# A hybrid state-space and conformer trunk: tables, backward scan, gates and z projections put into one hand-written TensorE order

## The chip, the cores and the metric

The kernel runs on one core of a Trainium2 chip. The metric is the time of one execution on the device in microseconds; the median of several runs is given. Every duration below is from one profiled execution. The engines are TensorE (PE in the rows, its weight loads PEld), VectorE (DVE), ScalarE (ACT) and GpSimd (POOL); SP issues most transfers.

## What is computed

Two layers run over 1024 latent tokens and 256 context tokens, 1024 features wide. The change lies in layer 0, whose mixer is this, cut to what matters:

```python
z, xbc, dt, glu, gate = split(h @ w_in)         # h: modulated tokens
# state-space branch, 16 heads, chunks of 128 tokens, 10 chunks in all
a_cum = cumsum(dt * a)                           # the tables, forward and backward
states = einsum(bc, exp(a_cum[-1] - a_cum), x*dt)
h_in = scan(h * exp(a_cum[-1]) + states)         # one scan forward, one backward
y = y_diag + y_off + flip(...) + x * d_skip
ya = rms_norm(y * silu(z))
# convolution branch
yb = silu(layer_norm(dwconv(val * sigmoid(gt), 31 taps))) * silu(gate)
out = concat([ya, yb]) @ w_out
```

## The kernel before

Each projection in 32-bit precision is three matmuls of a high and a low part: ScalarE casts the high part of a weight tile from its raw load (line 158: `wh`, `zh`, `woh`, `yh`), a subtraction on VectorE (line 159) makes the low part. Raw tiles (`wr`) have two buffers, which z weights and gate weights share.

The place is the end of `inproj0`. Up to there stand the glu and convolution-input projections, the early gates 4 to 7 (their Silu goes to DRAM as `gs_d`), and the long 31-tap convolution on GpSimd and VectorE. Then, in the program's order:

- `zblocks((0, 1))`: two of three blocks of the z and dt projection, ten token tiles each. Every tile of 352 columns takes 24 matmuls; between tiles stand transposes of conv output (`token_major`) and one modulation row at a time (`mod_row`, eight small matmuls on line 1308).
- `gate(2)`: one channel block of the gate projection, 72 matmuls over slices of 512, 512 and 256 tokens; ScalarE applies Silu (line 1384), GpSimd multiplies by the convolution output (line 1385).
- At the same time the conformer's normalisation (lines 928 to 939: statistics, eight subtractions on VectorE, eight activations), and the early gates: for each, `gs_d` is loaded into the one buffer `gse` (line 1331), multiplied on GpSimd (line 1332) and stored in three pieces (line 1334).
- `dt_prep`: the tables. A polynomial for dt on VectorE, `da` (line 1448), cumsum matmuls (lines 1453 to 1456), exponentials, casts into `xparts`, two sets of ten transposes (line 1495) and two transfers of the result (line 1497).
- `ssd_back`: the backward scan over ten chunks. For each, `xtok` is loaded (line 1511), scaled on VectorE (line 1515), multiplied in four `bst` matmuls (line 1535), added to the state (line 1539) and stored (line 1526).
- `zblocks((2,))`: the third z block. Its pool of split weights (`zp`) is opened after the pool with `gse` was closed and lies on the same memory.
- gates 3, 0 and 1, with loads of output weights `wb` (line 1406) after each, and the load and split of the first tile of the gated convolution (`yl0`, `yh0`, `ylo0`, line 1410 on).

Behind it `split_wo` casts seven output weights from `wb` and one from `xl`, and the forward scan runs interleaved with the output projection (line 1003).

A scheduler orders the instructions of each engine by its own estimates and by priorities, so the order in the program is not in every place that of an engine: in the kernel before, the scan matmuls and the z matmuls are mixed by it.

Of the kernel before, what the change touches and what calls it, by code (L numbers as in the profile page):

```python
# [90 lines left out]
def run(steps):  # L91

    for _ in steps:
        pass
# [16 lines left out]
class Kern:  # L111
# [1074 lines left out]
    def inproj0(self, hhi, hlo, cv, xbc_d, zs_d, gs_d, dtr, vwh, yb_d, xt_d, hb_d, s0, first):  # L1186
# [161 lines left out]
        def zblocks(js):  # L1348
            todo = [(c, h) for c in (1, 0, 9, 8, 7, 6, 5, 4, 3, 2) for h in range(2)]
            with ExitStack() as ez:  # L1350
                xq = ez.enter_context(self.pool(name="xq", bufs=2)) if js[0] < 2 else None
                zp = ez.enter_context(self.pool(name="zp", bufs=4))
                for j in js:
                    w = [self.load_w(zp, A["wzdt"][j, q], [P, 2, 352], "z", raw=(wp, "wr", [P, 8, P], 2)) for q in range(4)]
                    for t in range(NT):
                        ps = self.bank("mm")
                        ts = slice(t * P, (t + 1) * P)
                        self.mm3(ps[:, :352], (lambda k: hhi[:, k, ts], lambda k: hlo[:, k, ts]),
                                 (lambda k: w[k // 2][0][:, k % 2], lambda k: w[k // 2][1][:, k % 2]), range(8))
                        n = j * NT + t  # L1360
                        if 3 <= n < 2 * NT:
                            for _ in range(2 if n % 6 == 5 else 1):
                                token_major(xq, *todo.pop(0))
                        if mods:
                            layer, m, d, plus = mods.pop(0)
                            mod_row(layer, m, (23 - len(mods)) % 16)
                            if len(mods) == 8:
                                mod_turn(16, ((0, 16, self.gcol[:, 0], 0.0), (1, 0, self.mod1[:, 0], 0.0)))
                            elif not mods:
                                mod_turn(8, ((1, 8, self.mod1[:, 1], 1.0),))  # L1370
                        zs = tq.tile([P, 512], F32, name="zs", tag="th")
                        if j == 0:
                            nc.scalar.copy(dtr[:, t], ps[:, :32])
                            nc.scalar.activation(zs[:, :320], ps[:, 32:352], AF.Silu)
                            nc.sync.dma_start(zs_d[t, :, :320], zs[:, :320])
                        else:
                            nc.scalar.activation(zs[:, :352], ps[:, :352], AF.Silu)
                            nc.sync.dma_start(zs_d[t, :, 352 * j - 32:352 * j + 320], zs[:, :352])
                assert not xq or not todo

        def gate(i):
# [5 lines left out]

            self.proj_ch(wp, W[28 + i], hhi, hlo, ev)

        zblocks((0, 1))  # L1390
        gate(2)
        ecf.close()
        self.s0 = s0.__enter__()
        self.dt_prep(dtr)
        self.ssd_back(xt_d, hb_d)
        zblocks((2,))
        em.close()

# [3 lines left out]
        k = 0  # L1402
        for i, m in ((3, 3), (0, 5), (1, 7)):
            gate(i)
            for k in range(k, m):
# [10 lines left out]
    def dt_prep(self, dtr):  # L1416
# [3 lines left out]
        with ExitStack() as e:  # L1420
# [26 lines left out]
            for d in range(2):  # L1447
                nc.vector.scalar_tensor_tensor(
                    da[:, d], dt[:, :, 16 * d:16 * d + 16], -1.0,
                    ea[:, None, 16 * d:16 * d + 16].broadcast_to([P, NT, 16]), op0=ALU.mult, op1=ALU.mult)  # L1450
            ps = self.bank("ms")
            fl = da.rearrange("p d c h -> p d (c h)")
# [26 lines left out]
            for X, dst, quad in ((Ac, self.rA_d, False), (bias, self.rB_d, True)):  # L1479
# [8 lines left out]
                nc.vector.tensor_tensor(o(2).bitcast(FR), v(rem), o(1), op=ALU.subtract)  # L1488
                xq = xp.rearrange("p c t h -> p (c t h)")
                rt = q.tile([96, NT, P], F32, name="rt", tag="rt")  # L1490
                for j0 in range(0, NT, 4):
# [9 lines left out]
    def ssd_back(self, xt_d, hb_d):  # L1501
# [3 lines left out]
        with ExitStack() as e:  # L1505
# [15 lines left out]
            for i, c in enumerate(order):  # L1521
                xt, xs = nxt
                if i < len(order) - 1:
                    nxt = prep(order[i + 1])
# [157 lines left out]
```

## Time and profile before

| | us |
|---|---|
| median of 3 runs (2162.4 to 2163.54) | 2163.49 |
| the profiled execution's own time | 2159.51 |
| its span in the profile | 2157.5 |
| TensorE busy in the span | 2050.3 |

The span is what the profile shows from the first to the last instruction; 2.0 us of the execution's own time lie around it. Idle time of an engine matters only where the engines behind it wait for it; TensorE, busy 95% of the span, is the one on which most idle time counts.

### The profile page before, as it was taken

Reading aid. Unit: us, or ns where it says so; the run is one execution under the profiler, and the core shown is the slowest. Engines: PE = TensorE matmul, PEld = TensorE weight load, DVE = VectorE, ACT = ScalarE, POOL = GpSimd, SP = SyncE. Lnnn points to the kernel's source line nnn. Section 1 sums busy time; section 2 is a strip of 40 time slices with the busy share of each in tenths; the row PEclk is TensorE's granted clock in tenths of the full one; section 3 lists DMA queues with packets and bytes.
Section 4 is the critical chain, followed back from the end, with each engine's and each line's share of the span. In section 5 each row is a group of like instructions: output and inputs, shape, how many; then the busy total and the mean of one; then the engine's idle time right before and its main releaser. Section 6 shows DMA issues by size and latency. Waiting matters only on the chain. (4 is left out here: it accounts for less than half of the span.)

```text
span 2157.5 us, 28255 instructions
## 1 busy us (share of the span) xinstructions
PE 2050.3 (95%) x10636; PEld 1631.5 (76%) x10636; DVE 1344.7 (62%) x1889; ACT 990.9 (46%) x1549; POOL 980.0 (45%) x646
## 2 busy tenths in 40 slices
PE   7999999999995999999899999999999998899896
PEld 6888888889873876665588788888777776677675
DVE  6788897758454335678776221422566766676676
ACT  7455667543362132224233333333666877655510
POOL 0198999800222235556421114823345555434562
PEclk9999999999996999999899999999999999999998
DMA  8011122235756645555343322522312111533463
GB/s 311 30 40 33 47 87 79 88 131 191 234 161 203 241 144 176 179 190 175 120 147 113 129 71 98 186 83 84 101 48 67 51 47 48 157 112 115 145 179 127
DMA packets 156976, 268.01 MB, mean 124 GB/s; under 512 B 18677, under 2 KB 97393, under 8 KB 156585
## 3 DMA queue, kind: packets, MB, share of 16 engines
q1 hardware_dynamic: 155416, 262.69, 37.0%
q0 software_dynamic: 1280, 3.26, 0.5%
q8 instruction: 83, 1.36, 0.3%
q14 instruction: 53, 0.43, 0.1%
q10 hardware_dynamic: 144, 0.26, 0.0%
HBM read 189.17 MB, written 76.94 MB: 123 GB/s over the span
## 5 line engine op out<-in xcount | busy, mean ns | idle before, releaser
L1236 POOL TENSOR_TENSOR accq<-accq,prod 128x1295 f32<-128x1295 f32 x90 | 287.7, 3197 | 33.9 <-ACT prod L1235 17.2
L171 PE MATMUL m<-hhi,wh 128*128 128x512 f32 (+1 forms) x792 | 280.9, 355 | 1.8 <-ACT th L1279 0.9
L171 PE MATMUL m<-hlo,wh 128*128 128x512 f32 (+1 forms) x792 | 280.6, 354 | 0.0
L171 PE MATMUL m<-hhi,wl 128*128 128x512 f32 (+1 forms) x792 | 280.2, 354 | 0.0
L1244 DVE SCALAR_TENSOR_TENSOR acc<-u,vwh,acc 128x1295 f32<-128x1295 f32 x150 | 235.1, 1568 | 12.9 <-ACT acc L1241 9.7
L171 PE MATMUL m<-h1hi,wh 128*128 128x512 f32 (+1 forms) x544 | 213.2, 392 | 1.7 <-ACT rb L423 1.4
L733 POOL TENSOR_TENSOR pl<-pt,ph 128x512 fp32r<-128x512 f32 x96 | 129.3, 1349 | 186.2 <-ACT ph L732 178.7
L171 PE MATMUL m<-h1lo,wh 128*128 128x512 f32 (+1 forms) x544 | 213.0, 392 | 0.0
L171 PE MATMUL m<-h1hi,wl 128*128 128x512 f32 (+1 forms) x544 | 212.1, 390 | 0.0
L1003 PE MATMUL m<-wol,yh 128*128 128x512 f32 x448 | 182.1, 406 | 1.3 <-DVE wol L956 1.1
L1003 PE MATMUL m<-woh,yh 128*128 128x512 f32 x448 | 181.4, 408 | 1.8 <-ACT yh L158 0.9
L1003 PE MATMUL m<-woh,ylo 128*128 128x512 f32 x448 | 182.0, 406 | 0.3 <-DVE ylo L159 0.3
L1235 ACT ACTIVATE prod<-u,vwh 128x1295 f32<-128x1295 f32 x90 | 124.1, 1381 | 97.9 <-POOL accq L1236 95.6
L171 PEld LDWEIGHTS m<-hhi,wh 128*128 128x128 f32 x792 | 149.7, 189 | 24.1 <-ACT th L1279 1.6
L171 PEld LDWEIGHTS m<-hhi,wl 128*128 128x128 f32 x792 | 149.7, 189 | 20.8
L171 PEld LDWEIGHTS m<-hlo,wh 128*128 128x128 f32 x792 | 149.8, 189 | 20.6
L159 POOL TENSOR_TENSOR wl<-wr,wh 128x1024 fp32r<-128x1024 f32 x33 | 81.5, 2471 | 117.2 <-ACT wh L158 95.2
L732 ACT CAST ph<-pt 128x512 fp32r<-128x512 f32 x152 | 93.1, 619 | 81.5 <-PE po L740 70.4
L740 PE MATMUL po<-ph,vs 128*66 128x512 f32 x304 | 122.0, 401 | 3.8 <-ACT yo L745 3.8
L171 PEld LDWEIGHTS m<-h1hi,wh 128*128 128x128 f32 x544 | 102.7, 189 | 22.9 <-ACT rb L423 2.0
L171 PEld LDWEIGHTS m<-h1hi,wl 128*128 128x128 f32 x544 | 102.6, 189 | 21.0 <-issue 0.2
L171 PEld LDWEIGHTS m<-h1lo,wh 128*128 128x128 f32 x544 | 102.8, 189 | 19.7
(371 smaller groups left out, 4765.6 us busy)
## 6 DMA issues: line engine op xcount, KB each, us to landing
wr<-in_wch_dram SPq DMA_DIRECT2D x69, 512.0 KB
mw<-in_modw_dram SPq DMA_DIRECT2D x24, 512.0 KB
mr<-in_modw_dram SPq DMA_DIRECT2D x16, 512.0 KB
wor<-in_wout_dram SPq DMA_DIRECT2D x16, 512.0 KB
xbc_d<-acc SPq DMA_DIRECT2D x12, 640.0 KB
xcT<-xbc_d SPq DMA_DIRECT2D x20, 320.0 KB
xt_d<-xtok SPq DMA_DIRECT2D x20, 320.0 KB
xtok<-xt_d SPq DMA_DIRECT2D x10, 640.0 KB
```

Of the source, the lines that this page charges most:

```text
L159: (nc.gpsimd if pool_lo else nc.vector).tensor_tensor(lo, src, hi.bitcast(F32), op=ALU.subtract)
L171: nc.tensor.matmul(out, x(k), y(k), start=(c == 0), stop=(c == tot - 1))
L732: nc.scalar.copy(ph, p)
L733: (nc.gpsimd if x in (0, 1, 3) else nc.vector).tensor_tensor(pl, p, ph.bitcast(F32), op=ALU.subtract)
L740: nc.tensor.matmul(po[:66], vs[:, kb, v], p[y], start=first and i == 0, stop=last and i == 2)
L1003: nc.tensor.matmul(ps[f], y[u][:, k], w[k][v][:, 512 * f:512 * f + 512], start=i + j == 0, stop=i + j == 9)
L1235: nc.scalar.activation(pr, u[:, k:k + N], AF.Copy, scale=vwh[:, i, k:k + 1])
L1236: nc.gpsimd.tensor_tensor(acc, acc, pr, op=ALU.add)
L1244: nc.vector.scalar_tensor_tensor(acc[:, :N], u[:, k:k + N], vwh[:, i, k:k + 1], acc[:, :N], op0=ALU.mult, op1=ALU.add)
```

## The change

The stretch from gate 2 on gets a TensorE order written by hand (`manual_schedule` for that engine alone); the other engines stay with the scheduler. `zblocks`, `gate`, `dt_prep` and `ssd_back` become generators that hand back how many columns they have issued. `fill` yields the matmuls of gate 2, gate 3, then z block 2's weight loads, gate 0, and z block 2; `ahead` draws so many columns from it between the steps of the tables (15000, 16000, or up to the end of a gate) and of the backward scan (11700 for each chunk). Gate 1 stands behind. The modulation rows are drawn two at a time after each fifth tile of z blocks 0 and 1, and the turn of the last eight rows (`mod_turn`) comes after gate 2's matmuls. Loads of all seven `wb` come after gate 1. From line 1390 or so on, lines of the changed kernel stand 27 to 31 lower (the table transposes of line 1495 are line 1524, scan matmuls of line 1535 line 1565).

```diff
--- before.py
+++ after.py
@@ -1352,22 +1352,22 @@
                 zp = ez.enter_context(self.pool(name="zp", bufs=4))
                 for j in js:
                     w = [self.load_w(zp, A["wzdt"][j, q], [P, 2, 352], "z", raw=(wp, "wr", [P, 8, P], 2)) for q in range(4)]
+                    yield 0
                     for t in range(NT):
                         ps = self.bank("mm")
                         ts = slice(t * P, (t + 1) * P)
-                        self.mm3(ps[:, :352], (lambda k: hhi[:, k, ts], lambda k: hlo[:, k, ts]),
-                                 (lambda k: w[k // 2][0][:, k % 2], lambda k: w[k // 2][1][:, k % 2]), range(8))
+                        yield from self.mm3_(ps[:, :352], (lambda k: hhi[:, k, ts], lambda k: hlo[:, k, ts]),
+                                             (lambda k: w[k // 2][0][:, k % 2], lambda k: w[k // 2][1][:, k % 2]), range(8))
                         n = j * NT + t
                         if 3 <= n < 2 * NT:
                             for _ in range(2 if n % 6 == 5 else 1):
                                 token_major(xq, *todo.pop(0))
-                        if mods:
-                            layer, m, d, plus = mods.pop(0)
-                            mod_row(layer, m, (23 - len(mods)) % 16)
-                            if len(mods) == 8:
-                                mod_turn(16, ((0, 16, self.gcol[:, 0], 0.0), (1, 0, self.mod1[:, 0], 0.0)))
-                            elif not mods:
-                                mod_turn(8, ((1, 8, self.mod1[:, 1], 1.0),))
+                        for _ in range(2 if n % 5 == 4 and n < 20 else 1):
+                            if mods:
+                                layer, m, d, plus = mods.pop(0)
+                                mod_row(layer, m, (23 - len(mods)) % 16)
+                                if len(mods) == 8:
+                                    mod_turn(16, ((0, 16, self.gcol[:, 0], 0.0), (1, 0, self.mod1[:, 0], 0.0)))
                         zs = tq.tile([P, 512], F32, name="zs", tag="th")
                         if j == 0:
                             nc.scalar.copy(dtr[:, t], ps[:, :32])
@@ -1385,23 +1385,50 @@
                 nc.gpsimd.tensor_tensor(gt[:, :b - a], cv[i][:, a:b], gt[:, :b - a], op=ALU.mult)
                 nc.sync.dma_start(yb_d[a][i], gt[:, :b - a])
 
-            self.proj_ch(wp, W[28 + i], hhi, hlo, ev)
-
-        zblocks((0, 1))
-        gate(2)
+            return self.proj_ch_(wp, W[28 + i], hhi, hlo, ev)
+
+        run(zblocks((0, 1)))
         ecf.close()
         self.s0 = s0.__enter__()
-        self.dt_prep(dtr)
-        self.ssd_back(xt_d, hb_d)
-        zblocks((2,))
-        em.close()
+        with tc.manual_schedule(engines={mybir.EngineType.PE}):
+            def fill():
+                for i in (2, 3):
+                    yield from gate(i)
+                    yield None
+                z = zblocks((2,))
+                next(z)
+                yield from gate(0)
+                yield from z
+
+            def ahead(cols):
+                while cols > 0:
+                    c = next(oth, None)
+                    if c is None:
+                        return
+                    cols -= c
+
+            oth = fill()
+            dt = self.dt_prep(dtr)
+            next(dt)
+            ahead(15000)
+            mod_turn(8, ((1, 8, self.mod1[:, 1], 1.0),))
+            em.close()
+            ahead(99999)
+            next(dt)
+            ahead(16000)
+            next(dt)
+            ahead(99999)
+            run(dt)
+            for _ in self.ssd_back(xt_d, hb_d):
+                ahead(11700)
+            run(oth)
 
         ewl = self.ewl = ExitStack()
         wl = ewl.enter_context(self.pool(name="wl", bufs=1, side="right"))
         wb = [(k, wl.tile([P, D], F32, name=f"wb{k}", tag=f"wb{k}"), (wl, f"wb{k}")) for k in range(1, 8)]
         k = 0
-        for i, m in ((3, 3), (0, 5), (1, 7)):
-            gate(i)
+        for i, m in ((1, 7),):
+            run(gate(i))
             for k in range(k, m):
                 nc.sync.dma_start(wb[k][1], A["wout0"][9 + k])
             k = m
@@ -1448,6 +1475,7 @@
                 nc.vector.scalar_tensor_tensor(
                     da[:, d], dt[:, :, 16 * d:16 * d + 16], -1.0,
                     ea[:, None, 16 * d:16 * d + 16].broadcast_to([P, NT, 16]), op0=ALU.mult, op1=ALU.mult)
+            yield
             ps = self.bank("ms")
             fl = da.rearrange("p d c h -> p d (c h)")
             nc.tensor.matmul(ps[:, 0:160], self.tu, fl[:, 0], start=True, stop=True)
@@ -1487,6 +1515,7 @@
                 nc.scalar.copy(o(1).bitcast(FR), v(rem))
                 nc.vector.tensor_tensor(o(2).bitcast(FR), v(rem), o(1), op=ALU.subtract)
                 xq = xp.rearrange("p c t h -> p (c t h)")
+                yield
                 rt = q.tile([96, NT, P], F32, name="rt", tag="rt")
                 for j0 in range(0, NT, 4):
                     n = min(4, NT - j0)
@@ -1520,6 +1549,7 @@
             H = None
             for i, c in enumerate(order):
                 xt, xs = nxt
+                yield
                 if i < len(order) - 1:
                     nxt = prep(order[i + 1])
                 if H is not None:
```

No instruction of arithmetic is added or taken away; their orders on the engines are what differs. At three places:

TensorE at the tables and the start of the backward scan, before. `ms<-da` are the cumsums, `ms<-cs,xparts` the transposes of the tables, `ms<-cs,gcol` small matmuls that turn gate columns to rows, `bst` the scan, `m<-zh,hhi` z block 2:

```order
L1453 MATMUL ms<-da,cs 128x160
L1454 MATMUL ms<-da,cs 128x160
L1456 MATMUL ms<-da,cs 128x320
L1495 MATMUL ms<-cs,xparts 96x128 x20
L222 MATMUL ms<-cs,gcol 128x128 x8
L1535 MATMUL bst<-xtok 128x512 x6
L171 MATMUL m_5857<-zh,hhi 128x352
L171 MATMUL m_5895<-zh,hhi 128x352
```

And after, from gate 3's last matmuls (`m_5810`) on; `m_5900` is gate 0:

```order
L171 MATMUL m_5810<-hhi,wl 128x256
L171 MATMUL m_5810<-hhi,wh 128x256
L171 MATMUL m_5810<-hlo,wh 128x256
L171 MATMUL m_5810<-hhi,wl 128x256
L1524 MATMUL ms<-cs,xparts 96x128 x10
L222 MATMUL ms<-cs,gcol 128x128 x8
L171 MATMUL m_5900<-hhi,wh 128x512
L171 MATMUL m_5900<-hlo,wh 128x512
L171 MATMUL m_5900<-hhi,wl 128x512
L171 MATMUL m_5900<-hhi,wh 128x512
L171 MATMUL m_5900<-hlo,wh 128x512
```

The second set of transposes now has all of gate 3 ahead of it, and gate 0 stands ahead of the first scan matmul. Z block 2 starts only after gate 0 and among the scan.

GpSimd behind the convolution, before. `gs` are gate multiplications (`u_782` is gate 2, `u_783` gate 3), `gse` those of the early gates, `Hb` the backward scan's state:

```order
L1385 TENSOR_TENSOR gs<-u_782,gs 128x256
L1332 TENSOR_TENSOR gse<-u_784,gse 128x1280
L1332 TENSOR_TENSOR gse<-u_785,gse 128x1280
L1332 TENSOR_TENSOR gse<-u_786,gse 128x1280
L1332 TENSOR_TENSOR gse<-u_787,gse 128x1280
L1531 TENSOR_TENSOR Hb<-Hb,expS 128x1024 x4
```

And after:

```order
L1385 TENSOR_TENSOR gs<-u_782,gs 128x512
L1332 TENSOR_TENSOR gse<-u_784,gse 128x1280
L1385 TENSOR_TENSOR gs<-u_782,gs 128x256
L1385 TENSOR_TENSOR gs<-u_783,gs 128x512
L1332 TENSOR_TENSOR gse<-u_785,gse 128x1280
L1385 TENSOR_TENSOR gs<-u_783,gs 128x512
L1385 TENSOR_TENSOR gs<-u_783,gs 128x256
L1332 TENSOR_TENSOR gse<-u_786,gse 128x1280
L1332 TENSOR_TENSOR gse<-u_787,gse 128x1280
```

The three multiplications of gate 3 have moved in between those of the early gates; the scan's state still comes behind the last early gate.

ScalarE from the last gate to the output projection, before. `gs` is the Silu of gate 1, `yh_6489` the split of the first tile of the gated convolution, `woh` output weights, `g` the gate rows:

```order
L1384 ACTIVATE gs<-m_6395 128x512
L1384 ACTIVATE gs<-m_6424 128x512
L158 CAST yh_6489<-yl_6487 128x1024
L1384 ACTIVATE gs<-m_6453 128x256
L224 COPY g_6512<-ms 128x512 x2
L158 CAST woh_6516<-wb_6191 128x1024
L158 CAST woh_6520<-wb_6192 128x1024
L158 CAST woh_6524<-wb_6193 128x1024
L158 CAST woh_6528<-wb_6194 128x1024
```

And after (`yh_6492` is that same split):

```order
L1384 ACTIVATE gs<-m_6422 128x512
L1384 ACTIVATE gs<-m_6451 128x256
L224 COPY g_6515<-ms 128x512 x2
L158 CAST woh_6519<-wb_6380 128x1024
L158 CAST woh_6523<-wb_6381 128x1024
L158 CAST woh_6527<-wb_6382 128x1024
L158 CAST woh_6531<-wb_6383 128x1024
L158 CAST woh_6535<-wb_6384 128x1024
L158 CAST woh_6539<-wb_6385 128x1024
L158 CAST woh_6543<-wb_6386 128x1024
L224 COPY g_6516<-ms 128x512
L158 CAST yh_6492<-yl_6490 128x1024
```

The split of the first tile has moved from ahead of gate 1's last Silu to behind the seven output weights; the weights keep their order.

## Rows read from the trace of the kernel before

**Rows 1.** The page, busy time of each engine, its share and instructions

```profile
PE 2050.3 (95%) x10636; PEld 1631.5 (76%) x10636; DVE 1344.7 (62%) x1889; ACT 990.9 (46%) x1549; POOL 980.0 (45%) x646
```

**Rows 2.** Stretches: busy us (PE, PEld, DVE, ACT, POOL), clock, DMA share, GB/s

```profile
632.50:647.00 14.50, 10.01 (x71) 6.71 (x70) 13.83 (x23) 5.89 (x12) 6.48 (x5) 0.88 0.42 146
647.00:690.00 43.00, 17.58 (x53) 10.09 (x53) 13.77 (x18) 11.25 (x19) 12.41 (x5) 0.62 0.60 197
690.00:744.50 54.50, 52.30 (x278) 44.95 (x277) 28.38 (x45) 9.36 (x15) 13.50 (x7) 0.99 0.62 214
744.50:785.20 40.70, 40.70 (x214) 35.01 (x212) 1.23 (x1) 5.59 (x10) 10.04 (x8) 1.00 0.40 147
785.20:800.00 14.80, 12.58 (x61) 9.88 (x60) 11.12 (x10) 11.50 (x15) 4.71 (x3) 1.00 0.94 306
...
980.00:1065.00 85.00, 75.93 (x465) 45.02 (x464) 67.89 (x98) 32.64 (x50) 47.22 (x35) 0.90 0.36 122
```

**Rows 3.** Timeline of TensorE: start, us, line, operation, count, [idle before <-releaser]

```profile
632.61 3.65 PE L1308 MATMUL mz<-mw,scond 128*2 128x128 f32 x32
...
646.79 0.54 PE L1453 MATMUL ms<-da,cs 128*128 128x160 f32 x2 [1.87 <-DVE da L1448]
...
657.18 2.40 PE L1495 MATMUL ms<-cs,xparts 128*96 128x128 f32 x10 [9.04 <-DVE xparts L1488]
...
676.42 5.97 PE L1535 MATMUL bst<-xtok 128*128 128x512 f32 x8 [7.96 <-DVE xtok L1515]
```

**Rows 4.** Timeline of GpSimd, the multiplications of the early gates

```profile
641.03 2.89 POOL L1332 TENSOR_TENSOR gse<-u,gse 128x1280 f32<-128x1280 f32 x1 [0.25 <-ACT u L939]
651.18 2.88 POOL L1332 TENSOR_TENSOR gse<-u,gse 128x1280 f32<-128x1280 f32 x1 [7.26 <-DMA gse<-gs_d]
666.78 2.88 POOL L1332 TENSOR_TENSOR gse<-u,gse 128x1280 f32<-128x1280 f32 x1 [12.72 <-DMA gse<-gs_d]
678.86 2.89 POOL L1332 TENSOR_TENSOR gse<-u,gse 128x1280 f32<-128x1280 f32 x1 [9.20 <-DMA gse<-gs_d]
```

**Rows 5.** Timeline of ScalarE, 656 to 703 us

```profile
656.05 0.46 ACT L1487 CAST xparts<-tmpS 128x320 fp32r<-128x320 f32 x1 [1.14 <-DVE tmpS L1486]
...
688.35 1.46 ACT L158 CAST zh<-wr 128x704 fp32r<-128x704 f32 x2 [22.54 <-DMA yb_d<-gse]
696.73 0.78 ACT L158 CAST zh<-wr 128x704 fp32r<-128x704 f32 x1 [6.92 <-DMA wr<-in_wzdt_dram]
...
702.18 1.05 ACT L158 CAST wh<-wr 128x1024 fp32r<-128x1024 f32 x1 [2.62 <-DMA wr<-in_wch_dram]
```

**Rows 6.** Timeline of VectorE, the eight normalising subtractions

```profile
637.93 2.73 DVE L938 TENSOR_TENSOR u<-u,crp 128x256 f32<-128x256 f32 x8 [0.28 <-PE crp L935]
```

**Rows 7.** Timeline of SP, which issues the transfers

```profile
691.48 0.42 SPq L1152 DMA_DIRECT2D wr<-in_wzdt_dram  x1
...
698.46 0.33 SPq L1152 DMA_DIRECT2D wr<-in_wch_dram  x1
...
745.18 3.62 SPq L1406 DMA_DIRECT2D wb<-in_wout_dram  x5
```

**Rows 8.** TensorE by line and shape, 690 to 744.5 us: busy us, mean ns

```profile
L1535 PE MATMUL bst<-xtok 128*128 128x512 f32 x26 | 14.2, 636 | 0.3 <-DVE xtok L1515 0.3
```

**Rows 9.** Timeline of TensorE, end of gate 1, start of the output projection

```profile
784.98 0.28 PE L171 MATMUL m<-hhi,wl 128*128 128x256 f32 x1
...
789.46 0.50 PE L1003 MATMUL m<-wol,yh 128*128 128x512 f32 x1 [0.17 <-DVE wol L159]
```

**Rows 10.** Timeline of ScalarE, the same place

```profile
784.91 1.05 ACT L158 CAST yh<-yl 128x1024 fp32r<-128x1024 f32 x1 [1.84 <-DMA yl<-yb_d]
...
787.08 6.75 ACT L158 CAST woh<-wb 128x1024 fp32r<-128x1024 f32 x7
```

**Rows 11.** Timeline of VectorE, the same place

```profile
785.99 1.23 DVE L159 TENSOR_TENSOR ylo<-yl,yh 128x1024 fp32r<-128x1024 f32 x1 [26.07 <-ACT yh L158]
...
788.18 3.86 DVE L159 TENSOR_TENSOR wol<-wb,woh 128x1024 fp32r<-128x1024 f32 x3 [0.97 <-ACT woh L158]
```

## The prediction

> **What bounds the kernel now.** I read the page first: TensorE is busy 95% of the span [rows 1], so a stretch where it idles is where this change can gain. The table of stretches then shows one in its reach: from 632.5 to 690 us TensorE works 27.6 of 57.5 us, and the granted clock falls to 0.62, which lies between the two levels of 1.2 and 2.4 GHz [rows 2]. On both sides it is full: 52.3 of 54.5 us in z block 2, and 40.70 of 40.70 in gates 3, 0 and 1. So 30 us of idle time stand beside 93 us of projections that need nothing from the tables or the scan. That is the most that this change can be worth.
>
> TensorE's own rows show what makes the hole: the cumsums of the tables at 646.79, the transposes at 657.18 after 9.04 us of waiting for VectorE, the first matmuls of the scan (`bst`) at 676.42 after 7.96 us for scaled `xtok` [rows 3]. A second chain runs beside it, and ends later than one would think. The early gates 4 to 7 pass one by one through a single buffer, `gse`: load, multiplication on GpSimd, three stores. The multiplications start at 641.03, 651.18, 666.78 and 678.86, the last three after 7 to 13 us of waiting for the reload [rows 4]. The pool of z block 2's split weights lies on that buffer's memory. Hence ScalarE's first `zh` cast, 688.35, ends 22.54 us of idle time whose releaser is the last `gse` store [rows 5]. Today this costs little, since scan matmuls hold TensorE until 690.
>
> **The change, step by step.** The set of instructions is the same; only their order changes. I price the path that I take to set the end: tables, `gse` ring, `zh`, gate 0, z block 2, gate 1, then the output projection.
>
> (1) Start of the tables. Rows 20 to 23 of the modulation now stand ahead of gate 2 or in it. That is 64 matmuls on line 1308, 32 of which take 3.65 us, so gate 2 ends 7.3 us later, near 639.9 instead of 632.6 [rows 3]. The eight normalising subtractions (L938) started 5.3 us behind that end and took 2.73 us [rows 6]; shifted, they run from 645.2 to 647.9. VectorE's polynomial for dt now stands ahead of them, `da` behind. The cumsums come at 649, some 2 us later than now. Nothing is gained there: the tables waited for VectorE, not for TensorE.
>
> (2) The ring. Its first multiplication followed those subtractions by 0.4 us (641.03), so it moves to about 648.5. The second now stands behind gate 3's first multiplication in GpSimd's order. That one needs gate 3's first Silu, and ScalarE has the Silu behind the table cast that began 9.3 us after the cumsums and took 0.46 (656.05 against 646.79) [rows 3, 5]. 649 + 9.7 + 1.9 for Silu and its table load + 1.3 for the gate's product gives 661.9; it was 651.18. An unhindered round of the ring is 10.15 us (641.03 to 651.18), and gate 3's two other products stand in the way of the third: 673. The last round, with loads of `xtok` between on SP, takes its 12.08 us again: 685. From multiplication to `zh` were 9.49 us (678.86 to 688.35). So `zh` starts near 694.4, 6 us later than before [rows 4, 5]. Bounds: three unhindered rounds from 648.5 give 688.5; a third round as long as the slowest one (15.6 us) gives 699.
>
> (3) What is queued behind `zh`. `next(z)` stands ahead of gate 0, so in ScalarE's order four `zh` casts precede gate 0's two `wh` casts, and the raw weights of both go through the same two buffers. In the trace the first `wh` (702.18) follows the first `zh` by 13.83 us, with waits of 6.92 and 2.62 us for the loads [rows 5]. 1.5 us of that go: the third quarter's load was issued 3.1 us after `zh` (691.48), behind scan transfers on SP, where 1.6 us would do (two casts of 0.73 and subtractions like them) [rows 5, 7]. With the cast's 1.05 us gate 0 starts 13.4 us after `zh`, at 707.8. Gate 3's matmuls and the transposes among them are finished near 669.5 (649, plus 13.6 for the gate, plus 2.4 and 2.5 for transposes and about 2 for the rest). So the hole isn't filled but gathered: TensorE gets gate 3 into it, and then stands still for some 38 us. This is the step on which the forecast rests.
>
> The Trainium skill, "TensorE: Matmul & The Clock Gate", section "Architectural detail: the array is 16× 32×32, not 1× 128×128", says that ScalarE and VectorE work through their queues strictly in order, and that TensorE's queue lets weight loads alone pass. The `wh` wait of 2.62 us, with only `zh` and `wh` in the queue, agrees. Were it not so, gate 0 could start at 669.5.
>
> (4) The work from there. A gate is 13.6 us (40.70 / 3). Z block 2 with 26 of the 40 scan matmuls took 52.3 us [rows 2]; now all 40 stand in gate 0 and the z block. The 26 took 14.2 us by records that overlap, 0.55 each [rows 8]; I take 0.4, so 14 more cost 5.6, and 2.6 us of row turn and gate matmuls leave that stretch: 55.3. Gate 1 therefore ends at E = 707.8 + 13.6 + 55.3 + 13.6 = 790.3, against 785.26 (784.98 + 0.28) [rows 9]: **+5.0**.
>
> (5) The turn to the output projection. Before, `yh` was split at 784.91, ahead of the seven `woh` casts, and the subtraction `ylo` at 785.99 [rows 10, 11]. Now ScalarE has seven `woh` (6.75 us, from 1.8 us after gate 1's end) and one copy (0.5, half a cast by width) ahead of `yh` (1.05): E + 10.1. VectorE has `ylo` (1.23) ahead of all `wol` (3.86 / 3), so the first `wol` is done at E + 12.6. The third output matmul needs it; it started at 789.46, or E + 4.2 [rows 9]. **+8.4**, uncovered, since TensorE's order has nothing else there but 16 small matmuls for the gates' rows.
>
> (6) Small terms: the first matmuls after long idle time at a lower granted clock, **+0.5** (in the 632.5 to 690 stretch it was 0.62 to 0.88) [rows 2]. Given back later, **−2**: the forward scan's last chunks finish with 12 more output matmuls beside them, 2.8 us at 0.23 each, where TensorE idles 9.1 us in 980 to 1065 [rows 2].
>
> Sum: 5.0 + 8.4 + 0.5 − 2 = +11.9 on the profiled execution's 2159.5, or 2171.4. The median of the runs is 4.0 above that execution, so I predict **2175 us**.
>
> **The rivals.** (a) *The fill works.* If gate 0's weights don't wait for the ring's last store, gate 0 starts at 669.5, E is 752, 33 us earlier, and with step 5's +8.4 the time is 2159.5 − 33 + 8 + 4 = 2138. It decides in favour of faster once gate 0 starts 16.2 us earlier than forecast (the 11.9 us of the sum, and 4.3 for a difference that can be told), before about 691, which needs `zh` before 678. Against it is the row with 22.54 us; for it only the sight that loads of the gate's weights are small. In "Perfetto Trace Analysis", section "Optimization Strategy", the Trainium skill says that interleaving stages with different busiest engines may help. By that alone the result would be (a); no row here shows it for this place.
>
> (b) *No difference.* The ring keeps unhindered rounds (`zh` at 688.5, E at 784.4), and the 8.4 us of step 5 come back mostly in the 9.1 us of idle time of 980 to 1065, since the forward scan runs ahead of the output matmuls meanwhile. Then 2159.5 − 1 + 8.4 − 6 + 4 = 2165. For it: the scan needs little from `yh`. Against it: GpSimd's order puts gate 3's products into the ring.
>
> (c) *Slower still.* All seven `wb` loads now stand behind the last scan store and z block 2's end (E − 13.6) on SP; before, the last five were issued at 745.18 to 748.80, 37 us ahead of gate 1's end [rows 7, 9]. At the 306 GB/s of 785 to 800 each 0.52 MB takes 1.7 us and all are there in time; at 3.72 us each (the load of a gate's weights, 698.46 to 702.18) the seventh lands at E + 12.4 and `yh` at E + 15: 5 us more, 2180 [rows 2, 5, 7]. With the ring's upper bound (699) also 4.6 us: 2185.
>
> **How the numbers follow.** A measurement of this kernel can tell about 0.2%, 4.3 us, from no change. The forecast with (c) as its upper part, 0.68; (b) 0.15; (a), or half of it, 0.17. The range drops nearly all of (a), takes (b) in, and ends at the sum of the upper bounds: 2160 to 2187. The forecast's own range is 2169 to 2185. Slower holds 0.68, same 0.15, faster 0.17.
>
> **What would show it.** In the changed kernel's trace: cumsums near 649; the ring's multiplications at 648, 662, 673 and 685; an idle time of over 25 us of ScalarE ahead of `zh`, released by a `gse` store; TensorE idle from about 669 to 708, in one piece; gate 1's end near 790; then some 8 us until the first output matmul, which waits for `yh`. If gate 0 begins before 691, step 3 is wrong, and the kernel is faster. If gate 0 begins near 708 but the time is the same, the loss of step 5 was returned in the forward scan. If the output projection starts within 5 us of gate 1's end, I misread ScalarE's order.

## The result, and the profile after the change

The changed kernel takes 2179.09 us (median of 4, 2176.36 to 2181.16) against 2163.51 us of the kernel before run beside it: ratio 1.0075, interval 1.0062 to 1.0087. It is slower by 15.6 us, where 11.9 were forecast.

First the stretches of the changed kernel, with the columns of [rows 2]:

```profile
632.50:647.00 14.50, 9.53 (x38) 7.95 (x37) 12.61 (x34) 2.58 (x5) 2.95 (x4) 0.76 0.05 19
647.00:669.00 22.00, 20.27 (x121) 17.42 (x120) 13.00 (x20) 15.62 (x28) 10.71 (x6) 1.00 0.42 142
669.00:708.00 39.00, 7.36 (x32) 5.27 (x31) 8.38 (x8) 6.54 (x9) 6.48 (x3) 0.57 0.51 169
787.50:797.50 10.00, 2.55 (x21) 2.15 (x19) 0.23 (x1) 9.42 (x13) 1.83 (x2) 0.84 0.98 323
797.53:829.03 31.50, 26.87 (x101) 16.72 (x102) 29.14 (x28) 7.49 (x9) 15.06 (x7) 0.89 0.62 198
```

From 647 to 669 us TensorE is now nearly full, 20.27 us of 22.00, where it was busy 8.90 of them: gate 3 went into the hole. From 669 to 708 it is nearly empty, and a second hole stands at 787.5. TensorE's timeline shows what each waits for:

```profile
650.59 0.54 PE L1481 MATMUL ms<-da,cs 128*128 128x160 f32 x2 [0.44 <-DVE da L1475]
...
670.15 2.05 PE L222 MATMUL ms<-cs,gcol 128*128 128x128 f32 x16
703.46 0.80 PE L171 MATMUL m<-hhi,wh 128*128 128x512 f32 x1 [31.26 <-ACT wh L158]
...
709.08 0.40 PE L171 MATMUL m<-hhi,wh 128*128 128x512 f32 x1
...
787.72 0.28 PE L171 MATMUL m<-hhi,wl 128*128 128x256 f32 x1
789.00 2.05 PE L222 MATMUL ms<-cs,gcol 128*128 128x128 f32 x16 [1.00 <-ACT g L224]
797.53 1.22 PE L1003 MATMUL m<-woh,yh 128*128 128x512 f32 x2 [6.48 <-ACT yh L158]
800.05 0.79 PE L1003 MATMUL m<-wol,yh 128*128 128x512 f32 x1 [1.30 <-DVE wol L159]
```

Gate 0 waits 31.26 us for its weight `wh`. At 787.72 gate 1 has its last matmul, and the first output matmul comes at 797.53, released by `yh`. ScalarE's timeline has the reason for both:

```profile
692.69 1.46 ACT L158 CAST zh<-wr 128x704 fp32r<-128x704 f32 x2 [22.20 <-DMA yb_d<-gse]
...
702.36 1.04 ACT L158 CAST wh<-wr 128x1024 fp32r<-128x1024 f32 x1 [3.04 <-DMA wr<-in_wch_dram]
...
789.31 6.73 ACT L158 CAST woh<-wb 128x1024 fp32r<-128x1024 f32 x7
...
796.41 1.07 ACT L158 CAST yh<-yl 128x1024 fp32r<-128x1024 f32 x1
```

`wh` stands behind `zh`, which waits for the last store of `gse`; `yh` stands behind seven `woh`, which run without a wait, so the late `wb` loads had landed. SP's timeline adds that `wh` had nothing to cast before: the two buffers for raw weights (`wr`) held z block 2's first two from 625 us on, and gate 0's (one tile, as each gate has) was loaded only at 699.04, after the `zh` casts and their subtractions had freed a buffer.

```profile
625.12 3.43 SPq L1152 DMA_DIRECT2D wr<-in_wzdt_dram  x2
...
694.42 1.14 SPq L1152 DMA_DIRECT2D wr<-in_wzdt_dram  x2
...
699.04 1.56 SPq L1152 DMA_DIRECT2D wr<-in_wch_dram  x2
```

GpSimd's timeline, the early gates and the start of the output projection:

```profile
650.66 3.06 POOL L1332 TENSOR_TENSOR gse<-u,gse 128x1280 f32<-128x1280 f32 x1 [1.81 <-ACT u L939]
662.35 2.96 POOL L1332 TENSOR_TENSOR gse<-u,gse 128x1280 f32<-128x1280 f32 x1
675.05 2.88 POOL L1332 TENSOR_TENSOR gse<-u,gse 128x1280 f32<-128x1280 f32 x1 [5.27 <-DMA gse<-gs_d]
686.50 2.88 POOL L1332 TENSOR_TENSOR gse<-u,gse 128x1280 f32<-128x1280 f32 x1 [8.57 <-DMA gse<-gs_d]
...
799.93 2.36 POOL L159 TENSOR_TENSOR ylo<-yl,yh 128x1024 fp32r<-128x1024 f32 x1 [9.56 <-ACT yh L158]
802.25 2.89 POOL L1600 TENSOR_TENSOR tmp<-xt,wst 128x1024 f32<-128x1024 f32 x1
```

VectorE's timeline behind it:

```profile
797.51 1.23 DVE L159 TENSOR_TENSOR ylo<-yl,yh 128x1024 fp32r<-128x1024 f32 x1 [9.36 <-ACT yh L158]
798.77 7.45 DVE L159 TENSOR_TENSOR wol<-wb,woh 128x1024 fp32r<-128x1024 f32 x3
```

Three `wol` take 7.45 us here; they took 3.86 [rows 11].

**Where the time went.** Single executions of one kernel differ by some us (the first two profiles lie 21.7 us apart, the medians 15.6), so both kernels were profiled once more:

> The kernel before, unchanged, for a second profile. If the 275 us from its first output matmul to the last matmul of the forward scan belong to the kernel, they come again within 2 us; if the profiled execution was a lucky one, they are 278 or more.

> The changed kernel, unchanged, for a second profile. If the 284 us from its first output matmul to the last matmul of the forward scan belong to the kernel, they come again within 2 us; if the profiled execution was an unlucky one, they are 281 or less. The hole and the turn (gate 0 near 703.5, first output matmul 9.5 us behind gate 1's end) come again either way.

They took 2164.37 and 2181.0 us (spans 2162.5 and 2179.3). By the marks set there, the first profile of the kernel before was a lucky one, and the changed kernel's was not an unlucky one. Gate 1 ended at 786.59 and 789.10: **+2.5**. From there to the first output matmul were 3.4 and 9.5 us: **+6.1**. The third piece is the output stage, by which I mean everything from the first output matmul to the end of the forward scan. In the kernel before, second profile, as one stretch:

```profile
789.97:1068.90 278.93, 268.44 (x1498) 171.71 (x1497) 197.55 (x281) 87.47 (x128) 150.84 (x99) 0.96 0.51 168
```

In the changed one, second profile:

```profile
798.62:1083.60 284.98, 269.59 (x1495) 170.38 (x1496) 206.58 (x281) 82.82 (x121) 151.38 (x98) 0.95 0.47 158
```

That is **+6.1** more (+9 in the first two profiles, 276.0 and 285.2). The three make 14.7 of the spans' 16.8; the other 2.1 come later, and their cause is open. Nearly all of the third piece is lost at once. The first 31.5 us of the stage in the kernel before's first profile:

```profile
788.64:820.14 31.50, 30.25 (x117) 20.76 (x116) 20.64 (x29) 13.11 (x16) 14.71 (x9) 1.00 0.72 234
```

The row at 797.53 above is the same stretch of the changed kernel. TensorE's output matmuls in the two, by line and shape, before:

```profile
L1003 PE MATMUL m<-wol,yh 128*128 128x512 f32 x32 | 13.6, 425 | 0.2 <-DVE wol L159 0.2
L1003 PE MATMUL m<-woh,ylo 128*128 128x512 f32 x31 | 12.7, 410 | 0.0
L1003 PE MATMUL m<-woh,yh 128*128 128x512 f32 x32 | 11.6, 404 | 0.1
```

After, with the scan matmuls that waited (the 6.5 us lie ahead of the stage):

```profile
L1003 PE MATMUL m<-wol,yh 128*128 128x512 f32 x20 | 9.3, 463 | 2.4 <-DVE wol L159 2.4
L1003 PE MATMUL m<-woh,ylo 128*128 128x512 f32 x20 | 9.1, 454 | 0.0
L1003 PE MATMUL m<-woh,yh 128*128 128x512 f32 x21 | 8.6, 453 | 6.5 <-ACT yh L158 6.5
L1654 PE MATMUL po<-hbt,bcT 128*128 128x512 f32 x4 | 2.1, 618 | 1.7 <-DMA hbt<-hb_d 1.7
```

With the scan's own, 78 matmuls of 512 columns fall into the stretch where 111 did. The 33 missing ones are worth 7.5 us at 0.23 each; less 0.5 for the smaller matmuls that the changed kernel has more of there, some 7 us (an estimate). TensorE is busy 26.87 us instead of 30.25, mainly for waits on `wol` and on a load of the scan (`hbt`), and at a clock of 0.89 instead of 1.00.

### The profile page after: what moved, and what is told of

The parts are those of the page before. It is cut to its first block, busy times and chain, and to the rows that moved or that the text cites. A ratio compares the mean times of both kernels' runs of the same rounds, so it can differ in the third digit from the quotient of the medians.

```text
span 2179.4 us, 28252 instructions
## 1 busy us (share of the span) xinstructions
PE 2054.2 (94%) x10636; PEld 1634.0 (75%) x10636; DVE 1349.6 (62%) x1889; ACT 988.6 (45%) x1547; POOL 976.5 (45%) x646
## 5 line engine op out<-in xcount | busy, mean ns | idle before, releaser
L171 PEld LDWEIGHTS m<-hhi,wh 128*128 128x128 f32 x792 | 150.8, 190 | 55.9 <-ACT wh L158 31.5
```

Of the source, the lines that this page charges most:

```text
L171: nc.tensor.matmul(out, x(k), y(k), start=(c == 0), stop=(c == tot - 1))
```

## The experiments

The letters in the expectations: theory A is what the prediction says of the place, step 3 (gate 0's weights wait behind `zh` in ScalarE's order) in 1 and 3, step 5 (the late `yh`) in 2 and 4. E is the rival that the forward scan, by its own loads and order, takes back what is won ahead of it. B, C, D and H are rivals that are told where they stand. Theory G came after the first runs and stands ahead of experiment 7. Each kernel is timed against the kernel before, run beside it. The traces are of single executions: those of 4, 5 and 6 were 4.9, 4.5 and 9.2 us slower than the medians, that of 8 was 3.8 us faster, and their stages may share in that.

**1. Gate 0 ahead of z block 2's weights** (changed kernel, in `fill`).

```diff
+                yield from gate(0)
                 z = zblocks((2,))
                 next(z)
-                yield from gate(0)
                 yield from z
```

> The changed kernel with one exchange: gate 0 and its weights stand ahead of z block 2's weight loads, everything else as it is. Theory A (gate 0's weights wait only because the zh casts stand ahead of them in ScalarE's order, and those wait for the last gse store): gate 0 starts near 671 us instead of 703.5, z block 2 starts when zh is there, near 694.5, and gate 1 ends near 764 instead of 788; the time falls by about 22 us to 2157. Rival B (the hole is the scan's and the weights' own loads; gate 0 only exchanges its place with z block 2): gate 1 still ends at 785 or later, 2179.

2162.67 us, ratio 0.9993 [0.9982, 1.0003]. TensorE's timeline:

```profile
673.56 0.48 PE L171 MATMUL m<-hhi,wh 128*128 128x512 f32 x1
...
769.55 0.28 PE L171 MATMUL m<-hhi,wl 128*128 128x256 f32 x1
...
779.36 1.22 PE L1003 MATMUL m<-woh,yh 128*128 128x512 f32 x2 [6.48 <-ACT yh L158]
```

Gate 0 starts right behind the transposes, 30 us earlier, and the kernel is 16.4 us faster than the changed one: theory A holds for gate 0's start. Its price was too high (22 us, to 2157). The Trainium skill, "TensorE: Matmul & The Clock Gate", section "Architectural detail: the array is 16× 32×32, not 1× 128×128", says that ScalarE works its queue strictly in order. This run agrees with it, but does not test it alone: the exchange also gave gate 0's raw weights one of the two `wr` buffers early, so that the first `wh` was cast at 651.22 instead of 702.36. Yet gate 1 ends 16.8 us before that of the kernel before, and the time is the same. The wait for `yh` is still 6.48 us, and the output stage takes 290.0 us. So the fill can work, and 17 us are lost behind it: 6.2 up to the first output matmul, 11 in the stage.

**2. The turn by hand** (changed kernel: ScalarE and SP in a written order over gate 1; `wb` loads first, `yl` after gate 1's first slice, `yh` after the second).

```diff
...
+        for k in range(7):
+            nc.sync.dma_start(wb[k][1], A["wout0"][9 + k])
+        self.turn = tc.manual_schedule(engines={mybir.EngineType.Activation, mybir.EngineType.SP})
...
```

> The changed kernel with the turn to the output projection put back: ScalarE splits yh ahead of gate 1's last Silu and the woh casts, the load of yl stands right behind the first store of gate 1, and gate rows are copied after the casts; the hole stays. Theory A (the late yh costs what TensorE waits for it, uncovered): the first output matmul comes 3 to 4 us behind gate 1's end instead of 9.5, and the time falls by 6 to 9 us to 2171. Rival C (the forward scan gives the wait back later): within 2 us of 2179.

2175.92 us, 1.0053 [1.0041, 1.0065]: 3.2 us won of the 15.6, where theory A had 6 to 9. ScalarE's timeline, and what SP, which issues the load of `yl`, waited for:

```profile
792.31 1.04 ACT L158 CAST yh<-yl 128x1024 fp32r<-128x1024 f32 x1 [6.35 <-DMA yl<-yb_d]
```

```profile
SPq L1440 <- DMA yb_d<-gs: 5.9, 1, 5.9
```

`yh` now waits for its own load, and `woh` behind it. That load was issued only at 788.25, for it reads what gate 1's first slice stores, and SP waited 5.9 us for this store to land. The store was issued at 781.93, after the seven `wb` loads of 0.52 MB (774.21 to 778.47); that it lay behind their data is likely, but not shown. In the changed kernel the load of `yl` was issued at 787.65, so there too an earlier place for `yh` on ScalarE alone would not have given back all of the 6 us. The first output matmul comes 6.5 us behind gate 1's end here, and the stage takes 287.5 us.

**3. Three rounds of the ring** (the fourth early gate is neither loaded nor multiplied).

```diff
+            if i != early[-1]:
+                gt = aq.tile([P, 1295], F32, name="gse", tag="accq")
+                nc.sync.dma_start(gt[:, :T], gs_d[i])
+                nc.gpsimd.tensor_tensor(gt[:, :T], cv[i][:, :T], gt[:, :T], op=ALU.mult)
```

> The changed kernel without the fourth early gate's load and multiplication: the product of the third is stored in its place, so the ring has three rounds and that part of the output is another one. Theory A: the last gse store, the zh casts, gate 0 and gate 1's end all come about 11 us earlier (the distance of the last two multiplications, 675.05 to 686.50), and the time falls by about 11 us to 2168. Rival B (gate 0 waits for something else): the same time as the changed kernel, 2179.

2173.28 us, 1.0041 [1.0029, 1.0054]. `zh` came at 685.25, gate 0 at 696.27, and gate 1 ended 7.5 us earlier; the time fell by 5.8, not by 11. The ring sets the start of gate 0, a round is worth some 7 us, and the output stage (287.3) kept its loss.

**4. The kernel before, with `yh` behind the seven `woh`.** ScalarE has a written order from gate 1 to there; nothing else was moved by hand.

```diff
...
+        if vec is None and self.late:
+            for k, raw, slot in raws[:7]:
+                his[k] = wo.tile([P, D], FR, name=f"woh{k}", tag=f"woh{k}")
+                nc.scalar.copy(his[k], raw)
+            self.split(self.late[0], *self.late[1])
...
```

> The kernel before with the turn alone made as in the changed kernel: ScalarE casts the seven woh ahead of yh, wb loads and all else as before. Theory A: the third output matmul moves from 4.2 us behind gate 1's end to about 11, and the time grows by 6 to 9 us over the kernel before, to 2171. Rival C (given back in the forward scan): within 2 us of the kernel before. Rival D (what costs in the changed kernel are the late wb loads, which collide with the forward scan's loads, not the order on ScalarE): 0 to 2 us as well.

2178.07 us, 1.0072 [1.0060, 1.0084]. TensorE's timeline:

```profile
796.70 1.22 PE L1013 MATMUL m<-woh,yh 128*128 128x512 f32 x2 [8.07 <-ACT yh L158]
```

The kernel with the late `yh` is 14.7 us slower, nearly as much as with the whole change, though its projections stand where they stood and its `wb` loads are early. So C and D fall, and theory A's 6 to 9 us are too few. The third output matmul comes 12.3 us behind gate 1's end, where it came 4.2, and the output stage takes 288.5 us; 86 matmuls of 512 columns fall into its first 31.5. The scheduler made other orders of the other engines too, so the 14.7 us are those of the late `yh` with what follows from it.

**5. Experiment 1 with the turn by hand** (three `wb` loads, then `yl`, then four). **6. Gate 3 alone as filler**, gates 0 and 1 behind z block 2, and the turn by hand as in 2. First the edit of 5, then that of 6:

```diff
...
+        for k in range(3):
+            nc.sync.dma_start(wb[k][1], A["wout0"][9 + k])
+        self.turn = tc.manual_schedule(engines={mybir.EngineType.Activation, mybir.EngineType.SP})
...
```

```diff
-                z = zblocks((2,))
-                next(z)
-                yield from gate(0)
-                yield from z
+                yield from zblocks((2,))
...
```

> The changed kernel with both exchanges: gate 0 ahead of z block 2's weights, and the turn put back (yh ahead of gate 1's last Silu), with the loads in the order wb 1 to 3, yl, wb 4 to 7, so that yl does not queue behind all seven wb loads as it did when the turn alone was put back (yh waited 6.35 us for it there). Theory A (both losses stand by themselves): gate 1 ends near 770 as with gate 0 first, the first output matmul comes about 4 us later instead of 9.5, and the time is 6 us or more under that of the kernel with gate 0 first: 2150 to 2157, faster than before. Rival E (what follows the turn is set by the forward scan's own loads and order, so an earlier yh moves nothing): 2161 or more.

> The changed kernel with only gate 3 as filler of the hole: z block 2 with the scan (8500 columns a chunk) follows it, then gates 0 and 1 as in the kernel before, the seven wb loads right behind z block 2, and the turn put back. Theory A: z block 2 starts with zh near 694 and gate 1 ends near 777 (694.5 + 55 + 27.2), 8 us ahead of the kernel before; the wb loads have 27 us, yl lands in time, the first output matmul comes 3 to 4 us behind gate 1's end, and the time is about 2156. Rival E: the forward scan takes about 10 us longer again, and the time is 2163 or more.

2164.91 us, 1.0010 [0.9999, 1.0021], and 2163.59 us, 1.0004 [0.9994, 1.0014]. The first output matmul came 14.8 and 5.9 us before that of the kernel before (775.13 and 784.06 against 789.97), and all of it went in the output stage, 295.1 and 293.2 us. By the times, E holds. The traces show two different losses. In 6, TensorE's first 31.5 us lack about as much as in the changed kernel: `yh` is there, but TensorE waits for `woh` (2.0 us) and `hbt` (3.7), and the clock is 0.84. In 5 the output matmuls that stand ahead of the scan's end are used up at 991.7 us, and the scan's tail runs alone for 78.5 us; in the kernel before it does for 51.5, from 1013.1 on:

```profile
991.70:1070.22 78.52, 68.90 (x397) 37.47 (x397) 55.65 (x85) 22.34 (x38) 40.71 (x33) 0.72 0.30 100
```

```profile
1013.10:1064.60 51.50, 44.81 (x300) 26.12 (x301) 38.98 (x58) 16.20 (x28) 27.99 (x24) 0.83 0.31 102
```

So a turn put right by hand brought orders with losses of their own. These two runs do not tell the turn from the order of what follows it.

**Theory G** came of this. The `wb` tiles lie on the memory of z block 2's weights, so their loads can start only after that block: 752.99 in experiment 7, but 774.07 in the changed kernel, released by the block's last matmul, where gate 1 alone is left to hide them. The theory is that the scheduler, ordering by its own estimate of late loads, then puts `yh` behind `woh` and mixes output matmuls and scan in another way.

**7. Gate 3 as filler, gates 0 and 1 behind, `wb` loads between them**, and the turn left to the scheduler: the edit of 6 in `fill`, and

```diff
-                ahead(11700)
+                ahead(8500)
...
+        run(gate(0))
+        for k in range(7):
+            nc.sync.dma_start(wb[k][1], A["wout0"][9 + k])
+        run(gate(1))
```

> The changed kernel with gate 3 alone as filler, z block 2 with the scan (8500 columns a chunk) next, and gates 0 and 1 behind it, with the seven wb loads between the two gates in the program, and nothing else touched. The scheduler then gives the turn and the forward scan the order of the kernel before by itself (yh ahead of gate 1's last Silu; 152 output matmuls ahead of the first chunk's end). Theory G (the loss of the changed kernel lies in the order that late wb loads bring about, at the turn and in the forward scan): gate 1 ends near 778, the first output matmul comes 3.3 us later, the stage from there to the end of the forward scan takes 276 to 279 us as before, and the time is 2156, 7 us under the kernel before. Rival E (the forward scan always takes back what is won ahead of it): 2163.

2157.10 us, 0.9964 [0.9951, 0.9977]: 6.9 us faster than the kernel before. TensorE's timeline:

```profile
779.28 0.28 PE L171 MATMUL m<-hhi,wl 128*128 128x256 f32 x1
781.23 2.05 PE L222 MATMUL ms<-cs,gcol 128*128 128x128 f32 x16 [1.66 <-ACT g L224]
783.03 0.72 PE L1003 MATMUL m<-woh,yh 128*128 128x512 f32 x2
783.92 0.50 PE L1003 MATMUL m<-wol,yh 128*128 128x512 f32 x1 [0.17 <-DVE wol L159]
```

Output starts 3.5 us after gate 1, and the output stage as one stretch is that of the kernel before:

```profile
783.03:1060.80 277.77, 268.44 (x1498) 170.75 (x1497) 198.86 (x281) 87.52 (x128) 151.13 (x99) 0.96 0.52 169
```

**8. The changed kernel, and 9. experiment 1, with a `memset` in place of the seven `wb` loads.**

```diff
-                nc.sync.dma_start(wb[k][1], A["wout0"][9 + k])
+                nc.gpsimd.memset(wb[k][1], 0.0)
```

> The changed kernel with the seven wb loads left out and the tiles set to zero by GpSimd, so that part of the output is another one; the hole and gate 0 stay. The scheduler, with no late loads, gives the turn and the forward scan the order of the kernel before. Theory G: gate 1 ends at 788 as in the changed kernel, but the first output matmul comes 3.3 us later instead of 9.5, the stage from there to the end of the forward scan takes 276 to 279 us instead of 285, and the time falls to about 2166. Rival H (the hole and gate 0's delay make the loss): 2177 or more.

> The same without wb loads (part of the output is another one) on the kernel with gate 0 ahead of z block 2's weights. Theory G: gate 1 ends near 770, and turn and forward scan run as in the kernel before: 788.6 - 773 = 15 us under it, 2148. Rival E (the forward scan takes back what is won ahead of it, whatever the order): 2160 or more.

2164.41 us, 0.9996 [0.9986, 1.0006], and 2148.26 us, 0.9921 [0.9907, 0.9935]. TensorE's timeline of 8:

```profile
703.58 0.80 PE L171 MATMUL m<-hhi,wh 128*128 128x512 f32 x1 [30.66 <-ACT wh L158]
...
788.06 0.28 PE L171 MATMUL m<-hhi,wl 128*128 128x256 f32 x1
...
791.73 0.71 PE L1003 MATMUL m<-woh,yh 128*128 128x512 f32 x2
```

The hole of 31 us is still there, yet the turn is short again and the time is that of the kernel before. So nearly all of the loss hangs on the `wb` loads; the hole by itself moves gate 1's end by some 2.5 us. That the loads act by the orders made of them, and not by their transfers, these two runs alone do not show; experiment 4, where the loads are early and the loss is there, speaks for the orders. In 9, where the hole is filled too, a gain of the kind of rival (a) appears, 15.7 us. Both output stages (273.0 and 277.0) also lack the real weights' values and transfers, so a few us of them may be due to that.

**10. Experiment 7 with the first slice of gate 0 in the hole.**

```diff
+                for _ in range(25):
+                    yield next(g0)
                 yield from zblocks((2,))
```

> The kernel with gate 3 as filler, z block 2, and gates 0 and 1 behind, plus the first slice of gate 0 (24 matmuls, 5.4 us) ahead of z block 2 in the hole; the order of turn and forward scan stays that of the kernel before. Theory G: gate 1 ends as much earlier as the slice is long, if zh keeps its start near 694: 5 us, and the time is 2152. Theory G with a later zh (with all of gate 0 there it came at 701 instead of 693): no gain over 2157. Rival E: no gain.

2155.00 us, 0.9961 [0.9947, 0.9974]: no difference from experiment 7 that can be told. `zh` moved to 698.91 (691.46 there), which took back most of the slice; gate 1 ended only 1.6 us earlier. These two are the best complete versions.

The runs side by side: how many output matmuls stand ahead of the last matmul of each of the first four chunks in TensorE's order, and the output stage of the profiled execution.

```
kernel                         ahead of chunks 1 to 4    stage us
before; 7; 8; 9; 10            152 234 290 350    276 to 279; 277.8; 273.0; 277.0; 275.3
changed                        117 184 252 312    285.0
1                              151 211 284 353    290.0
2 and 6                        177 240 300 364    287.5, 293.2
3                              144 215 297 387    287.3
4                              154 223 301 370    288.5
5                              201 261 333 402    295.1
```

The kernels of the first line have nearly the same order on all four compute engines, and all of them keep the short stage; all others differ from it on all four, and lose 6 us or more. The counts themselves do not decide: 1 and 4 have nearly those of the kernel before. Which engine's order costs the time was not separated.

## Why the prediction was right, and where not

**The path (steps 1 to 3)** was right from the ring on. The cumsums came at 650.59 (forecast 649), the ring's multiplications at 650.66, 662.35, 675.05 and 686.50 (648.5, 661.9, 673, 685), gate 0 at 703.46 (707.8). The 4.3 us less came behind the last multiplication: `zh` followed in 6.2 us instead of 9.49, and `wh` led gate 0 10.8 us after `zh`, not 13.4, since no scan transfers stood between on SP. Step 3 also named the two raw buffers, rightly (of its two `wh` casts the second is gate 1's, which changes nothing in the sum); the 2.62 us that it cites for ScalarE's strict order do not show it, for the row ends that wait with the load of `wh`'s own raw weights [rows 5]. In step 1 the reasoning failed, and the time came out near by luck: gate 2 ended at 650.15, not 639.9, since none of its matmuls ran from 633.1 to 641.1, around the turn of the modulation rows. The normalising subtractions did not wait for its end, but started at 647.56 within it.

**Step 4** was too large by its start: gate 1's end moved by 2.5 to 2.7 us, not 5.0. From gate 0 on the work took 84.5 us (703.46 to 788.00) where 82.5 were reckoned. The clock, for which step 6 had 0.5, is worth that much: the first twelve matmuls of gate 0 took 5.6 us at 0.51 to 0.80 each (703.46 to 709.08), the next ones 0.39 and 0.23 apart.

**Step 5** was right in ScalarE's and VectorE's order. The third output matmul came 12.05 us after gate 1's end (12.6 forecast), +7.9 against +8.4.

**Step 6 is the term that failed.** "Given back later, −2" assumed that the scan running ahead would return time. Nothing was returned: in the second profiles the stage lost 4.4 us more behind its third matmul, where step 5's account ends, and 2.1 came behind the stage. The loss lies at the stage's start: some 7 us in its first 31.5, of which 1.6 belong to step 5's third matmul. There `wol` made TensorE wait (1.30 us at 800.05 and more behind it), a load of the scan did, and the clock was at 0.50 after the wait for `yh`. The prediction priced none of this, apart from the 0.5 for the clock. Experiment 4 has such a loss with the late `yh` and early loads (86 matmuls of 512 columns there); experiment 7, with `yh` early and the order of the kernel before, does not (109, against 111 in the kernel before); by how much each of the waits and the clock carries it is open.

Summed up on the second profiles: 2.5 for gate 1's end where 5.5 were reckoned with the clock, 7.8 for the turn where 8.4, and 6.5 behind it where −2, together 16.8 against 11.9. Two errors cancelled in part, so that the medians' 15.6 lie only 3.7 above the sum; that is luck.

**The rivals.** (a) was refuted for this change, and its mechanism confirmed by experiments 1 and 9; its price was not, for in 1 `zh` itself came later (701.36) and gate 1 ended at 769.8, not 752. (b) fell with step 6: nothing was given back on balance. (c) named the right suspects, the seven `wb` loads, by the wrong mechanism. No `woh` waited for them; by theory G they act through the order that the scheduler makes of them. Why the scheduler does so is inferred from its orders: it was not read from its estimates.

## What to carry to other kernels

Work drawn into a hole fills it only if its operands don't queue behind something that waits for the hole's own end: follow each filler's first load and cast through its engine's queue, the raw buffers that it shares, and the memory it lands on. Where a scheduler orders the rest, the work that is pulled forward was also the cover of later loads, and a stage far behind can come out in another order; price that stage from the compiled order, not as unchanged. Look at the order also where the loads come in time: with two gates (27 us) between the buffers' release and the first use the scheduler kept its order, with one (13.6 us) it did not, though no cast waited for its load.

## What was not expected of the hardware

A subtraction `wol` of 128x1024 takes VectorE 1.23 us. The second and third of the seven took 3.35 and 2.81 us, and just then GpSimd ran `ylo` and `tmp` (799.93 to 805.14, above); in the kernel before the first three kept to 3.86 us together. The Trainium skill, "SBUF — State Buffer", section "Who interferes with whom", says that a VectorE instruction with two inputs in SBUF contends with a GpSimd instruction that reads SBUF. These rows agree: moving `yh` also moved GpSimd's work onto the subtractions that TensorE waited for, and the two slow ones cost VectorE 3.7 us.

After idle time the clock costs more than I gave it: 5.6 us for twelve matmuls behind the 31 us hole (granted clock 0.50, the lower level of 1.2 GHz, from 703.46 to 707 us, and 0.51 up to 709), where the next ones follow each other every 0.23 us, 2.7 for twelve. At the start of the output stage, after a wait of 6.48 us, it was 0.50 again, 1.2 GHz, from 797.53 to 804 us.
